# Retention operands of a hybrid encoder block: split before they are stored, or after they are loaded

## The chip, the core and the metric

The kernel runs on one core of one Trainium2 chip. Five engines work side by side, each with its own instruction queue in program order: TensorE (PE, with its weight loads shown as PEld), VectorE (DVE), ScalarE (ACT), GpSimd (POOL) and SyncE (SP), which here only issues DMAs. The metric is the device time of one launch in microseconds, as the median of several runs. One further execution was profiled, and the views of its trace are what the text reads.

## The reference

One encoder layer over 2048 rows of width 1024. After an RMS norm one matrix product gives ten groups of columns. Branch A is a banded attention over chunks of 64 rows. Branch B is a retention with 8 heads, keys of width 64 and values of width 128. Both are gated, projected, merged, projected again, added to the input and normed. What the change touches is branch B:

```python
qr = rotary(q_r.reshape(B, S, R_HEADS, R_KEY_DIM), positions)
kr = rotary(k_r.reshape(B, S, R_HEADS, R_KEY_DIM), positions)
o_r = retention_chunkwise(qr, kr, v_r.reshape(B, S, R_HEADS, R_VAL_DIM), gn_gain[l])
...
s = jnp.einsum('bnqhd,bnkhd->bnhqk', qc, kc) * intra_decay
o_intra = jnp.einsum('bnhqk,bnkhe->bnqhe', s, vc)
kv = jnp.einsum('bnkhd,hk,bnkhe->nbhde', kc, state_decay, vc).astype(jnp.float32)
...
return state * chunk_decay[None, :, None, None] + kv_n, state
...
mean = jnp.mean(o, axis=-1, keepdims=True)
var = jnp.mean(jnp.square(o - mean), axis=-1, keepdims=True)
o = (o - mean) * lax.rsqrt(var + GN_EPS)
```

Rotated queries and keys make scores, scores and a running state make the output, and each head's output is normed over its 128 values. The kernel centres the values over these 128 ahead of time, so that the output needs no mean.

## The kernel before

**Numbers in two halves.** Matrix products take operands in the type fp32r, which holds fewer bits than fp32. To keep the accuracy, an operand is split: the high half is a cast to fp32r on ScalarE, the low half is the fp32 number less the high half, on VectorE or GpSimd. A product of two split numbers is three matmuls, or two where the halves of one operand lie under each other in the partitions.

**Stages.** The rows are handled in two halves s = 0, 1 of 1024 rows, two blocks b of 512 rows in each. For every half the stages are: the projection of queries, keys and values (`p0`, `p1`: 14 chunks of 256 columns, by a Strassen scheme of seven products), attention, and retention. The projections of the gates (`g0`, `g1`) run along with attention and retention: their products are cut into steps of three matmuls of 512 columns, and `fill(n)` (L497) puts n such steps between the parts of attention or retention. A credit carries fractions over, so 1.9 means 19 steps in ten fills. At the end come the merge and the output projection.

**Deferred work.** `later(n, fn)` (L242) defers a piece of work by n steps; `step()` (L487) first emits what is due, then the next three matmuls. `put(lag, dst, src)` is a deferred store. `emit` takes the earliest piece out of the list, and `sure(cond)` (L1493) emits pieces in order until its condition holds. In these stages every engine keeps the order in which the pieces are emitted; all DMAs but the weight loads are issued on SP, in that order.

**Buffers.** The pool `E` holds tiles of 128 x 512 fp32, 23 of them in a projection and 22 in retention (`E_PROJ`, `E_RET`). An instruction that writes a new tile waits until its buffer's last use is over; for a load that wait stands in SP's queue. PSUM has four banks `ACC`, shared by the gate products and the kv update.

**Queries and values before they are stored.** A block of rotated queries is two tiles `xs` (first and second half of the rotary pairs). `parted` (L936) casts each to a high half, makes the low half, and stores both: four stores of 256 KB for a block and a group of four heads. Values: `ep_vr` (L985) transposes them, subtracts the mean (`centred`), casts the high half on ScalarE (`high`), makes the low half on GpSimd (`low`), and stores both: two stores of 256 KB for a head and a block.

**Retention** (`retention`, L1364) goes through `todo`: for each pair p of heads four steps st of 256 rows. An item is one head i of a step. `load_scored` loads keys `kr`, queries `qr` (each row twice, once under the other, since the keys' halves lie so) and, at a pair's first step, the masks `dm`. `load_valued` loads decayed keys `kd` and values `vr`. For each item, `scores` makes the matmuls into `sr`, then `sm` = `sr` times the mask on VectorE, `sh` its high half on ScalarE and `sl` its low half on GpSimd; they are used two items, or four fills, later by `output`. `update` makes the matmuls `kv`, and its `added` brings them into `state` [64 x 256]: at st = 0 ScalarE copies, else VectorE scales and adds, and then VectorE adds three more parts. Three steps later ScalarE casts the high half of the state into `sstk`, one step later VectorE makes the low half. In the first half's last step of a pair (st = 3) the state is stored to `sts` and `sks` for the second half, three steps later still. `evacuate` takes the output from PSUM, squares it and sums the squares on TensorE (`ssq`). The loop at L1568 sets the order:

```python
if st < 7:
    update(p, st)
if m + 1 < len(todo):
    load_valued(*todo[m + 1])
```

Both stand at a step's start (i = 0), ahead of the fill; the scored loads of the step after next stand at the end of its first item.

Of the kernel before, what the change touches and what calls it, by code (L numbers as in the profile page):

```python
# [21 lines left out]
P = 128  # L22
# [48 lines left out]
def hybrid_kernel(  # L71
# [881 lines left out]
    def queries(cc, b, xs, nm, late):  # L953
        parted(xs, nm, late + 9, dve, lambda i, h: r32(qrscr[cc][b][:, :, :, h, i]).rearrange("u i c t -> (i c) u t"))
# [30 lines left out]
    def ep_vr(cc, b, j, src, ps):  # L985
# [4 lines left out]
        def rest():  # L990
# [4 lines left out]
            vv = []  # L995
# [17 lines left out]
            later(4, high)  # L1013
            later(6, low)
# [349 lines left out]
    def retention(s, ps_ret):  # L1364
# [8 lines left out]
        def load_scored(p, st):  # L1373
# [5 lines left out]
            qs = []  # L1379
# [5 lines left out]
            for i in range(2):  # L1385
                q = E(f"qr_{nm}_{i}", F32R, (P, 2, T))
                for half in range(2):
                    dma(
                        r32(q[64 * half:64 * half + 64]),
                        r32(qrscr[cc][b][un, 2 * (p % 2) + i]).rearrange("c h n t -> (c h) n t"),  # L1390
                    )
                qs.append(q)
                if st == 4 * s:
                    load_mask(p, i)
            tiles[p, st] = ks, qs

        def load_valued(p, st):

            b, un = st // 2, st % 2
            nm = f"{p}_{st}"  # L1400
            kd = E(f"kd_{nm}", F32R, (P, 2, T))
            dma(r32(kd), r32(kdscr[p][b][:, un]))
            vs = []
            for i in range(2):
                v = E(f"vr_{nm}_{i}", F32R, (P, 2, 2 * DV))
                dma(
                    r32(v), r32(vrscr[2 * p + i][b][:, 2 * un:2 * un + 2]).rearrange("p t n d -> p t (n d)")
                )
                vs.append(v)
            values[p, st] = vs, kd.rearrange("p i (t c) -> p i t c", t=2)  # L1410

# [11 lines left out]

        def scores(p, st, i):

            nm = f"{p}_{st}_{i}"
            ks, qs = tiles[p, st]
            sp = ps_ret.tile([P, 512], F32, tag="sr", bufs=2, name=f"sr_{nm}")
            for kk in range(2):
                o = sp[:, kk * T:(kk + 1) * T]  # L1430
                kcol = ks[:, i, kk * P:(kk + 1) * P]
                pe.matmul(o, kcol, qs[i][:, 0, :], start=True, stop=False)
                pe.matmul(o, kcol, qs[i][:, 1, :], start=False, stop=True)
# [19 lines left out]
        def update(p, st):  # L1453

            vs, kd = values[p, st]
            kv = ACC(f"kv_{p}_{st}")
# [36 lines left out]
        def sure(here):  # L1493

            while not here():
                emit()

        def output(p, st, i, parts, ops):
            qs, vs = tiles[p, st][1], values[p, st][0]
            o = ops[:, i * T:(i + 1) * T]  # L1500
            sure(lambda: len(parts) == 2 and (st == 0 or (p, st) in sstks))
# [284 lines left out]
```

## Time and profile before

| what | us |
|---|---|
| median of 3 runs | 1989.13 (1988.7 to 1997.05) |
| the profiled execution: time | 1994.13 |
| the profiled execution: span of the trace | 1992.3 |
| mean granted TensorE clock | 0.994 |
| DMA issues `qr<-qrs`, x128 of 128 KB: median to landing | 4.4 |
| DMA issues `vr<-vrs`, x64 of 256 KB: median to landing | 5.3 |
| bytes moved by DMA | 447.45 MB, mean 225 GB/s |

A view's row names engine, operation, and what it writes and reads by the program's tile names; `x64` counts instructions. Nearly all rows carry line 140, that of the helper through which every engine call goes, so instructions are told apart by their tiles. Tiles that end in `_p` and `_g` belong to the q/k/v and gate projections. The retention stages lie at about 590 to 780 and 1365 to 1565 us from the start of the span, the two q/k/v projections at 0 to 366 and 780 to 1130.

### The profile page before, as it was taken

How to read it: one execution, taken by the hardware profiler on the slowest of the kernel's cores; microseconds unless marked ns; L12 is line 12 of the kernel's file. 1: busy time of each engine (PE TensorE's matmuls, PEld its weight loads, DVE VectorE, ACT ScalarE, POOL GpSimd, SP SyncE). 2: the span in 40 equal slices, each digit the busy share in tenths (PEclk: the TensorE clock that was granted, in tenths of full speed). 3: DMA queues.
4: the chain of work that ended last, by engine and by line, in shares of the span. 5: the costliest groups of instructions: out<-in, count | busy, mean ns of one | idle time of the engine just before them, and what ended most of it. 6: DMA issues, size and time to landing. Idle time of an engine off the chain costs nothing.

```text
span 1992.3 us, 30382 instructions
## 1 busy us (share of the span) xinstructions
PE 1927.1 (97%) x9712; PEld 1606.7 (81%) x9712; DVE 1362.2 (68%) x2613; ACT 900.4 (45%) x1827; POOL 853.0 (43%) x703
## 2 busy tenths in 40 slices
PE   6899999999999999999999999999999999999998
PEld 4677788888887877787788888888888887888886
DVE  7887878677765658889887677765557653544554
ACT  6454554566654545443333555654455311322221
POOL 2343544555546665555553444444665144021000
PEclk9999999999999999999999999999999999999999
DMA  4576795756549987687785646554998999976564
GB/s 148 156 265 186 226 307 196 213 153 183 161 132 268 289 243 250 214 289 230 231 277 173 190 150 176 157 144 141 275 285 283 334 377 360 341 242 216 193 193 138
DMA packets 341967, 447.45 MB, mean 225 GB/s; under 512 B 30808, under 2 KB 195312, under 8 KB 341808
## 3 DMA queue, kind: packets, MB, share of 16 engines
q1 hardware_dynamic: 284800, 389.92, 61.3%
q10 hardware_dynamic: 57008, 55.59, 9.2%
q8 instruction: 78, 1.28, 0.3%
q14 instruction: 81, 0.66, 0.1%
HBM read 294.50 MB, written 150.89 MB: 224 GB/s over the span
## 4 chain that ended last, share of the span: by engine, by line
PE 52%; DMA 6%; DVE 6%; issue 2%; POOL 1%; SPq 1%; ACT 0%; DVEq 0%; ACTq 0%; POOLq 0%
PE ps_g_z L140 4%; PE ps_g_x L140 4%; PE ps_p_z L140 3%; PE o L140 2%; PE po L140 2%; PE ps_p_x L140 2%; PE ps_g_v L140 2%; PE ps_g_w L140 2%; PE ps_g_y L140 2%; PE wide L140 2%; PE tp L140 1%; PE ps_p_y L140 1%; PE sr L140 1%; PE ps_p_w L140 1%; PE ps_p_v L140 1%
## 5 line engine op out<-in xcount | busy, mean ns | idle before, releaser
L140 POOL TENSOR_SCALAR pr<-pr,rsum 128x640 f32<-128x640 f32 (+4 forms) x128 | 96.0, 750 | 225.9 <-DVE ptl L140 105.7
L140 PE MATMUL ps_p_z<-r,wh_p 128*128 128x512 f32 x448 | 142.7, 400 | 7.0 <-DVE c_p L140 4.5
L140 PE MATMUL ps_g_z<-r,wh_g 128*128 128x512 f32 x448 | 143.9, 403 | 4.0 <-DVE c_g L140 4.0
L140 PE MATMUL ps_g_x<-r,wh_g 128*128 128x512 f32 x448 | 142.7, 400 | 1.9 <-ACT u_g L140 1.9
L140 PE MATMUL ps_p_x<-r,wh_p 128*128 128x512 f32 x448 | 142.3, 399 | 1.4 <-ACT u_p L140 1.4
L140 DVE CUSTOM_DVE_ANT_0 pr<-wide,bt 128x640 f32<-128x640 f32 (+4 forms) x128 | 94.3, 737 | 71.2 <-PE wide L140 65.4
L140 ACT ACTIVATE pr<-pr,mn 128x640 f32<-128x640 f32 (+4 forms) x128 | 98.0, 766 | 84.9 <-DVE mn L140 84.9
L140 POOL TENSOR_TENSOR t_p<-raw_p,t_p 128x512 f32<-128x512 f32 x50 | 74.5, 1491 | 130.1 <-DVE wl_p L140 114.9
L140 DVE TENSOR_TENSOR ptl<-tp,pth 128x384 fp32r<-128x384 f32 x168 | 96.0, 573 | 40.8 <-ACT pth L140 40.5
L140 ACT CAST pth<-tp 128x384 fp32r<-128x384 f32 x168 | 84.7, 516 | 70.0 <-PE tp L140 64.5
L140 DVE TENSOR_TENSOR wl_p<-t_p,wh_p 128x512 fp32r<-128x512 f32 x112 | 106.4, 951 | 2.0 <-ACT wh_p L140 2.0
L140 POOL TENSOR_TENSOR sl<-sm,sh 128x512 fp32r<-128x512 f32 x64 | 87.7, 1371 | 44.3 <-ACT sh L140 27.5
L1122 POOL TENSOR_TENSOR gr<-gr,ta 128x512 f32<-128x512 f32 x32 | 44.6, 1395 | 141.8 <-DVE gr L1121 133.3
L140 PEld LDWEIGHTS ps_p_z<-r,wh_p 128*128 128x128 f32 x448 | 82.5, 190 | 24.7 <-issue 7.2
L140 PEld LDWEIGHTS ps_p_x<-r,wh_p 128*128 128x128 f32 x448 | 83.8, 190 | 19.9 <-ACT u_p L140 2.2
L140 PE MATMUL wide<-ka,qa 128*128 128x512 f32 (+2 forms) x448 | 94.4, 326 | 2.3 <-DVE mn L140 2.3
L140 DVE TENSOR_TENSOR sm<-sr,dm 128x512 f32<-128x512 f32 x64 | 44.1, 690 | 71.9 <-PE sr L140 41.3
L140 PEld LDWEIGHTS tp<-ident,pr 128*128 128x128 f32 x560 | 71.3, 140 | 27.1 <-POOL pr L140 2.2
L140 POOL TENSOR_TENSOR wl_g<-t_g,wh_g 128x512 fp32r<-128x512 f32 x56 | 75.0, 1339 | 42.3 <-ACT wh_g L140 31.4
L140 PE MATMUL po<-pth,va 128*128 128x256 f32 x336 | 93.1, 298 | 0.0
L140 PE MATMUL tp<-ident,pr 128*128 128x128 f32 x560 | 89.0, 272 | 2.9 <-POOL pr L140 1.6
L140 ACT CAST wh_p<-t_p 128x512 fp32r<-128x512 f32 x112 | 69.1, 619 | 48.1 <-PE ps_p_z L140 19.5
(1184 smaller groups left out, 5879.2 us busy)
## 6 DMA issues: line engine op xcount, KB each, us to landing
raw_g<-in_w_in_dram ACTq DMA_DIRECT2D x56, 512.0 KB, 5.4
raw_p<-in_w_in_dram ACTq DMA_DIRECT2D x50, 512.0 KB, 6.4
qa<-qas SPq DMA_DIRECT2D x128, 128.0 KB, 3.1
qr<-qrs SPq DMA_DIRECT2D x128, 128.0 KB, 4.4
vr<-vrs SPq DMA_DIRECT2D x64, 256.0 KB, 5.3
ka<-kas SPq DMA_DIRECT2D x40, 256.0 KB, 3.7
va<-vas SPq DMA_DIRECT2D x40, 256.0 KB, 3.4
kds<-kdt_k SPq DMA_DIRECT2D x32, 256.0 KB, 4.4
```

Source lines behind the costliest of these rows:

```text
L140: return tc.keep_in_program_order(op(*a, **k))
L1122: pool.tensor_tensor(g, g, ta, ALU.add)
```

## The change

Queries and values are stored whole, as fp32, and split in retention after they are loaded. A query tile now holds both heads of a pair, each row twice as before, and is split into a high tile (ScalarE) and a low one in place (VectorE); values come as one tile for both heads, and their high halves (ScalarE) and low halves (VectorE) go into two tiles. The splits are deferred by 7 or 8 steps from the load, and by more at retention's start; `sure` now also guards scores, update and output until the splits are emitted. Values of the step after next are loaded at the end of a step, scored loads at a step's start. The update's matmuls come behind the fill. `state` is set to zero by GpSimd at a pair's start in place of ScalarE's copy, and VectorE makes both halves of the state at once behind the sums. The diff, cut to its core:

```diff
-    qrscr = [[D(f"qrs_{c}_{b}", [2, 4, 32, 2, 2, T], F32R) for b in range(NB)] for c in range(2)]
+    qrscr = [[D(f"qrs_{c}_{b}", [2, 2, 32, 2, 2, T]) for b in range(NB)] for c in range(2)]
-    vrscr = [[D(f"vrs_{h}_{b}", [P, 4, 2, DV], F32R) for b in range(NB)] for h in range(HEADS)]
+    vrscr = [[D(f"vrs_{h}_{b}", [P, 4, DV]) for b in range(NB)] for h in range(HEADS)]
...
     def queries(cc, b, xs, nm, late):
-        parted(xs, nm, late + 9, dve, lambda i, h: r32(qrscr[cc][b][:, :, :, h, i]).rearrange("u i c t -> (i c) u t"))
+        def store(n, i):
+            src = xs[n][32 * i:32 * i + 32].rearrange("c (u t) -> c u t", u=2)
+            dma(qrscr[cc][b][:, i // 2, :, n, i % 2].rearrange("u c t -> c u t"), src)
+        for n in range(2):
+            for i in range(4):
+                later(late + 8 + PUT + n, lambda n=n, i=i: store(n, i))
...
-            def high():
-                vv.extend(two(f"vr_{nm}", (P, 4, DV)))
-                act.copy(vv[0], vc)
-            def low():
-                pool.tensor_tensor(vv[1], vc, r32(vv[0]), ALU.subtract)
-                for n in range(2):
-                    put(PUT, r32(vrscr[h][b][:, :, n, :]), r32(vv[n]))
+                put(PUT, vrscr[h][b], vc)
...
-        def load_scored(p, st):
+        def load_scored(p, st, more=0):
...
+            ql = E(f"qr_{nm}", F32R, (P, 2, T))
+            for half in range(2):
+                dma(
+                    r32(ql[64 * half:64 * half + 64]),
+                    qrscr[cc][b][un, p % 2].rearrange("c h i t -> (c h) i t"),
+                )
...
+            def high():
+                qs.append(E(f"qh_{nm}", F32R, (P, 2, T)))
+                act.copy(qs[0], r32(ql))
+                later(2, low)
+            def low():
+                dve.tensor_tensor(ql, r32(ql), r32(qs[0]), ALU.subtract)
+                qs.append(ql)
+            later(8 + more, high)
-        def load_valued(p, st):
+        def load_valued(p, st, more=0):
...
+            raw = E(f"vr_{nm}", shape=(P, 2, 2, DV))
+            for i in range(2):
+                dma(raw[:, i], vrscr[2 * p + i][b][:, 2 * un:2 * un + 2])
...
+            def high():
+                ws = [E(f"v_{nm}_{i}", F32R, (P, 2, 2 * DV)) for i in range(2)]
+                for i in range(2):
+                    act.copy(ws[i][:, :, 0:DV], raw[:, i])
+                later(2, lambda: low(ws))
+            def low(ws):
+                for i in range(2):
+                    dve.tensor_tensor(ws[i][:, :, DV:2 * DV], raw[:, i], r32(ws[i][:, :, 0:DV]), ALU.subtract)
+                vs.extend(ws)
+            later(7 + more, high)
...
             def added():
                 for i in range(2):
-                    if st == 0:
-                        act.copy(state[:, i, :], kvv[0:64, i, 0:DV])
-                        continue
...
-                later(3, lambda: high(sstk))
-            def high(sstk):
-                act.copy(sstk[0:64], state)
-                later(1, lambda: low(sstk))
-            def low(sstk):
+                dve.tensor_copy(sstk[0:64], state)
                 dve.tensor_tensor(sstk[64:128], state, r32(sstk[0:64]), ALU.subtract)
                 if st == 3:
                     put(3, stscr[p], state.rearrange("p i c -> p (i c)"))
...
-        load_scored(*todo[0])
-        load_valued(*todo[0])
-        load_scored(*todo[1])
+        load_scored(*todo[0], 3)
+        load_valued(*todo[0], 5)
+        load_scored(*todo[1], 5)
         load_state(*todo[0])
+        load_valued(*todo[1], 9)
+        load_scored(*todo[2], 9)
...
-                if st < 7:
-                    update(p, st)
                 if m + 1 < len(todo):
-                    load_valued(*todo[m + 1])
                     load_state(*todo[m + 1])
+                if m and m + 2 < len(todo):
+                    load_scored(*todo[m + 2])
             fill(RET_FILL)
+            if i == 0 and st < 7:
+                if st == 0:
+                    pool.memset(state, 0.0)
+                update(p, st)
...
-            if i == 0 and m + 2 < len(todo):
-                load_scored(*todo[m + 2])
+            if i == 1 and m + 2 < len(todo):
+                load_valued(*todo[m + 2])
             fill(RET_FILL)
```

More of the change, by code (lines that the diff above doesn't have):

```diff
@@ L1422, in load_mask, with sure @@
             dma(dms[p][i], dmask[2 * p + i])
+        def sure(here):
+            while not here():
+                emit()
         def scores(p, st, i):
@@ L1431, in scores @@
                 kcol = ks[:, i, kk * P:(kk + 1) * P]
-                pe.matmul(o, kcol, qs[i][:, 0, :], start=True, stop=False)
-                pe.matmul(o, kcol, qs[i][:, 1, :], start=False, stop=True)
+                pe.matmul(o, kcol, qs[0][:, i, :], start=True, stop=False)
+                pe.matmul(o, kcol, qs[1][:, i, :], start=False, stop=True)
             got = []
@@ L1500, in output @@
             o = ops[:, i * T:(i + 1) * T]
-            sure(lambda: len(parts) == 2 and (st == 0 or (p, st) in sstks))
+            sure(lambda: len(parts) == 2 and len(vs) == 2 and (st == 0 or (p, st) in sstks))
             sh, sl = parts
@@ L1504, in output @@
                 sstk = sstks[p, st]
-                pe.matmul(o, sstk[:, i, :], qs[i][:, 0, :], start=True, stop=False)
-                pe.matmul(o, sstk[:, i, :], qs[i][:, 1, :], start=False, stop=False)
+                pe.matmul(o, sstk[:, i, :], qs[0][:, i, :], start=True, stop=False)
+                pe.matmul(o, sstk[:, i, :], qs[1][:, i, :], start=False, stop=False)
             for kk in range(2):
```

27 lines of the change are left out of this document (5 added, 22 removed).

## The prediction

> **What bounds the kernel now.** First the head of the page: which engine is full. Then the busy time of each engine in long stretches that follow the stages (columns: stretch, length, busy time and instructions of PE, PEld, DVE, ACT and POOL, granted clock, DMA share, GB/s).
>
> ```profile
> span 1992.3 us, 30382 instructions
> PE 1927.1 (97%) x9712; PEld 1606.7 (81%) x9712; DVE 1362.2 (68%) x2613; ACT 900.4 (45%) x1827; POOL 853.0 (43%) x703
> ```
>
> ```profile
> 20.00:366.00 346.00, 329.56 (x1523) 266.03 (x1522) 274.68 (x405) 178.01 (x375) 149.25 (x102) 0.99 0.66 209
> 590.00:780.00 190.00, 180.07 (x1009) 154.12 (x1007) 114.77 (x194) 93.84 (x181) 112.95 (x84) 0.99 0.84 254
> 780.00:1130.00 350.00, 340.52 (x1569) 278.15 (x1570) 293.96 (x405) 145.60 (x277) 181.36 (x127) 1.00 0.75 239
> 1365.00:1565.00 200.00, 197.91 (x1114) 170.37 (x1113) 122.48 (x207) 101.20 (x188) 112.67 (x84) 1.00 0.86 267
> ```
>
> TensorE bounds it: it is idle for 65 us of 1992. The change leaves every matmul and touches four stages: the two q/k/v projections (20 to 366 and 780 to 1130), where work goes, and the two retentions (590 to 780 and 1365 to 1565), where work comes. There PE is idle for 16.4, 9.5, 9.9 and 2.1 us. So 38 us, part of it start-up, is all that could be won; the question is how much of it this change ends, and how much it makes. Next, what PE waited for: three rows of the whole run, five of the first retention, one of the second (us, times, longest).
>
> ```profile
> PE ps_p_z L140 <- DVE c_p L140: 4.5, 4, 1.6
> PE trva L140 <- DVE c_p L140: 2.4, 3, 1.1
> PE ps_p_w L140 <- DVE wl_p L140: 2.1, 3, 1.0
> ```
>
> ```profile
> PE ps_g_z L140 <- DVE c_g L140: 2.1, 1, 2.1
> PE ps_g_x L140 <- ACT u_g L140: 1.9, 2, 1.2
> PE o L140 <- POOL sl L140: 1.7, 3, 1.0
> PE kv L140 <- DMA vr<-vrs: 1.3, 2, 0.8
> PE ssq L140 <- POOL o2l L140: 1.1, 1, 1.1
> ```
>
> ```profile
> PE kv L140 <- DMA vr<-vrs: 0.4, 1, 0.4
> ```
>
> The longest is 2.1 us at 723; the timeline (start, length, idle before and its releaser) tells why.
>
> ```profile
> 710.69 3.16 SPq L140 DMA_DIRECT2D qr<-qrs  x4
> ...
> 716.44 0.47 SPq L140 DMA_DIRECT2D sts<-state  x1
> ...
> 720.59 0.42 ACT L140 COPY state<-kv 64x128 f32<-64x128 f32 x2 [3.82 <-DMA sts<-state]
> 721.04 1.33 DVE L140 TENSOR_TENSOR state<-kv,state 64x256 f32<-64x256 f32 x3 [5.29 <-ACT state L140]
> ...
> 723.15 0.74 PE L140 MATMUL ps_g_z<-r,wh_g 128*128 128x512 f32 x2 [2.06 <-DVE c_g L140]
> ```
>
> A new head pair starts. ScalarE's copy into `state` must wait until the store of the last pair's state has read it; VectorE waits for ScalarE, the gate sum c_g stands behind VectorE's state parts, and PE waits for c_g. The other rows I need give retention's rate: two kv updates four steps apart, an output beside them, and two stretches.
>
> ```profile
> 661.49 0.48 PE kv L140 x4
> ...
> 663.34 0.96 PE o L140 x8
> ...
> 696.82 0.48 PE kv L140 x4
> ```
>
> ```profile
> 660.00:700.00 40.00, 40.00 (x244) 35.37 (x244) 23.29 (x46) 22.84 (x46) 27.11 (x22) 1.00 0.93 283
> 720.00:740.00 20.00, 17.94 (x100) 15.53 (x99) 13.17 (x25) 11.67 (x23) 9.52 (x7) 0.91 0.75 225
> ```
>
> A step (one pair, 256 rows) takes (696.82 - 661.49)/4 = 8.83 us; sixteen take 141 us. Where PE never idles (660 to 700), VectorE is busy for 58%, or 5.14 us of a step, and DMA for 93%.
>
> **The change part by part.** *Store wait at a new pair.* The store was due 1+3+1+3 = 8 steps behind the update, the next pair's first sum 8.6 behind it (four fills of 1.9, and one): no room. (These are steps of the projection, 7.6 to a retention step.) Now VectorE does both halves at once, so the store is due after 4 and the memset that must wait for it after 7.6: 3.6 steps of 8.83/7.6 us = 4.2 us later, and the store above took 720.59 - 716.44 = 4.1 us. I count the wait as gone: 2.06 us, and with it the lower clock behind it, 0.09 of 20 us (0.91 in that slice) = 1.8 us. Gain 3.9 us, bounds 0 and 3.9. If the SP queue is late, GpSimd waits in ScalarE's place (a rival).
>
> The Trainium skill ("TensorE: Matmul & The Clock Gate", What's actually happening) has the clock fall after an idle window of about 3.4 us. Here the slice behind an idle time of 2.06 us has 0.91. By the page alone this part would be worth 2.1 us and not 3.9; the measurement decides.
>
> *Loads issued earlier.* Scores' loads move ahead of a fill, and so ahead of that fill's gate and output stores on SP; these stores free buffers only. Four query loads took SP 3.16 us above, two remain, 1.6 us less a step, which pays for it. Values are asked for at the end of the step two before their use. The kv waits, 1.3 + 0.4 = 1.7 us, go; their splits are due 9 steps after the load, 2.4 before use, so these hide. Gain 1.7, bounds 0 and 1.7.
>
> ```profile
> L140 DVE TENSOR_TENSOR l_q<-u_p,h_q 128x512 fp32r<-128x512 f32 x8 | 5.4, 679 | 0.0
> L140 POOL TENSOR_TENSOR l_vr<-u_p,h_vr 128x512 fp32r<-128x512 f32 x16 | 21.1, 1320 | 0.0
> L140 ACT CAST h_vr<-u_p 128x512 fp32r<-128x512 f32 x16 | 9.9, 620 | 12.9 <-DVE u_p L140 12.9
> ```
>
> *Projections relieved.* Out go 16 splits of queries and 32 of values: on VectorE 16 x 0.68 = 11 us, on GpSimd 32 x 1.32 = 42 us, on ScalarE 48 x 0.62 = 30 us, half of each per projection. VectorE holds PE up there for 4.5 + 2.4 + 2.1 = 9.0 us. It loses 11 of 569 us, and GpSimd, which makes it wait, 42 of 331. I take a quarter of the 9.0: gain 2.3, bounds 0 and 9.0. Query stores go from 4 to 8 per block of 512 rows and column group, value stores from 2 to 1 per head: with two groups and eight heads SP has 24 a block before and after.
>
> *DMA.* 64 of the 128 query loads of 128 KB go, the 64 value loads halve, the stores halve: 8.4 + 8.4 + 4.2 + 8.4 = 29 MB of 447. In the rows above PE waits for DMA at kv alone. So this is worth nothing beyond the two parts above, unless the full queue causes more than its rows say.
>
> *Splits that come into retention.* For VectorE per step: one query low half (128x512), two value low halves (128x256), one state copy (64x256); at a pair's first step also two scaled adds in place of copies. None of these is in retention's trace; the nearest rows, 600 to 757:
>
> ```profile
> L140 DVE TENSOR_TENSOR wl_g<-raw_g,wh_g 128x512 fp32r<-128x512 f32 x14 | 12.8, 912 | 0.0
> L140 DVE TENSOR_TENSOR state<-kv,state 64x256 f32<-64x256 f32 x48 | 20.3, 423 | 11.6 <-ACT state L140 10.1
> L140 DVE TENSOR_TENSOR sstk<-state,sstk 64x256 fp32r<-64x256 f32 x16 | 10.4, 650 | 1.6 <-ACT sstk L140 1.2
> L140 DVE SCALAR_TENSOR_TENSOR state<-state,kv 64x128 f32<-64x128 f32 x24 | 5.7, 274 | 8.5 <-PE kv L140 8.5
> ```
>
> The query half: 0.68 (l_q) to 0.91; I take 0.91, the same shape in the same stage. A value half has 256 columns and two SBUF operands like sstk: 0.42 to 0.65, I take 0.65, twice. The copy: 0.2 (half of 0.42) to 0.65, I take 0.42. The adds: 2 x 0.27 in one step of four, 0.14. Together 0.91 + 1.30 + 0.42 + 0.14 = 2.8 us (1.9 to 3.5 if every SBUF operation meets GpSimd as the worst of these did): VectorE goes from 58% to 7.9/8.83 = 90%. ScalarE gets three casts for one, at most 3 x 0.62 = 1.9 us a step: from 57% (22.84 of 40) to at most 78%; not the bound.
>
> The Trainium skill ("SBUF — State Buffer", Who interferes with whom) says why 0.65 and not 0.42: a VectorE operation with two SBUF operands and a GpSimd operation that reads SBUF lock each other out, one with a PSUM operand does not. The rows agree (650 against 423 ns). It speaks against this change: all four new operations would be of the blocking sort, and by it GpSimd would be held up too, a cost that my sum leaves out.
>
> What does 90% cost? PE against VectorE in the second projection:
>
> ```profile
> 780.00:830.00 50.00, 46.58 (x192) 36.75 (x193) 48.97 (x55) 28.03 (x51) 32.83 (x20) 0.97 0.72 237
> 830.00:1030.00 200.00, 195.74 (x902) 160.04 (x901) 173.83 (x228) 74.86 (x142) 109.03 (x73) 1.00 0.82 266
> ```
>
> ```profile
> 1525.00:1545.00 20.00, 19.71 (x115) 16.78 (x113) 18.84 (x29) 12.69 (x26) 10.18 (x6) 1.00 0.85 279
> ```
>
> At 87% PE idles 4.26 of 200 us, 2.1%; at 98%, 3.42 of 50, 6.8%. Thirty-two steps are about 295 us: 2.1% is 6.2 us. Of the waits that stay (1.9 + 1.7 + 1.1) some are the same ones, so loss 4.0, bounds 0 and 20. The second retention's end is at 94% already: loss 1.0, bounds 0 and 3.
>
> *The query split is tight in the first retention.* Scores come 5 fills x 1.9 = 9.5 steps after the load, the low half is due after 10. In about half of the 16 steps it is issued directly ahead of the scores. If a gate sum (0.69) stands before it on VectorE, PE comes 0.69 + 0.91 - 0.96 (the output) = 0.64 us early. Products end every fourth step: between 2 and 4 such meetings, loss 1.5, bounds 0 and 8 x 0.64 = 5.1. With 2.2 a fill in the second retention there is room.
>
> Sum: -3.9 - 1.7 - 2.3 + 4.0 + 1.0 + 1.5 = **-1.4 us** on the profiled 1994.13 (span 1992.3 and 1.8 around it), which lies 5.0 above the median of the runs, 1989.13. From the median: **1987.7**.
>
> **The rivals.** *A: the queue costs more than its rows say.* SP's loads and stores are in order, DMA stands at 93%; with fewer of them ScalarE and GpSimd get theirs earlier too, and the other waits of the first retention (1.9 + 1.7 + 1.1 = 4.7) go as well, while VectorE's 42% of free time takes the splits. For it: nearly all retention's waits sit in the first, with three new pairs. Against: none of the 4.7 names a DMA. 7.9 + 4.7 = 12.6 less: 1976.5.
>
> *B, slower: VectorE fills up.* Place: retention's steps, where state sums, gate sums and masks queue behind the splits. It decides from 98% on: 0.98 x 8.83 - 5.14 = 3.5 us added a step, the upper end above. Price 6.8% of 295 = 20.1, less the 7.9: 2001.3. Against: the masks' results are used four fills later.
>
> *C: the wait moves to GpSimd.* If the state store is issued 4 us late (SP blocked by a load without a free buffer), the memset waits, and the score low halves behind it on GpSimd, and PE for these. The gain of 3.9 is lost, and two more pairs stall alike: -1.4 + 3 x 3.9 = +10.3: 1999.4.
>
> *D: the loads are issued sooner but do not start sooner*, because they wait for a free buffer of the 22: kv's 1.7 stays: 1989.4.
>
> **How the numbers follow.** Forecast 0.44, A 0.24, B 0.18, C 0.06, D 0.08. About 0.5% (10 us) is what a measurement of this kernel can tell from no change. Faster than that: A, 0.24. Within: forecast and D, 0.52. Slower: B and C, 0.24. The range goes to the middle of A and of B and a little beyond: 1974 to 2002.
>
> **What would show it.** VectorE's share in 660 to 700 near 90% (under 80% speaks for A, 97% for B); no PE wait for vr at kv; no long wait of VectorE for `state` at a new pair, and a memset on GpSimd that waits for the store would be C; 418 MB moved, DMA share in retention near 0.75; fewer PE waits for c_p in the projections; short PE waits of the scores (sr) for VectorE in the first retention alone. Wrong would be the forecast if PE's idle time in the two retentions together left the stretch from 4 to 18 us.

## The result, and the profile after

| | before | after |
|---|---|---|
| median of 5 runs, us | 1989.13 | 2008.01 |
| lowest to highest, us | 1988.03 to 1997.05 | 2006.79 to 2008.88 |
| the profiled execution: time, us | 1994.13 | 2008.28 |
| its span, us | 1992.3 | 2006.4 |

The ratio is 1.0087, with a 95% interval of 1.0067 to 1.0106: slower by 0.9%. The forecast was 1987.7, its range 1974 to 2002, so the time lies outside the range, on the side of rival B. The head of the page of the changed kernel, and the same long stretches as before:

```profile
span 2006.4 us, 30244 instructions
PE 1935.0 (96%) x9712; PEld 1611.6 (80%) x9712; DVE 1437.5 (72%) x2729; ACT 897.0 (45%) x1839; POOL 817.2 (41%) x675
```

```profile
20.00:366.00 346.00, 331.52 (x1530) 267.63 (x1530) 270.73 (x398) 164.75 (x351) 126.33 (x86) 0.99 0.60 192
590.00:780.00 190.00, 176.53 (x975) 150.04 (x974) 161.25 (x255) 100.80 (x200) 116.08 (x87) 0.98 0.65 202
780.00:1130.00 350.00, 340.34 (x1560) 277.69 (x1559) 284.82 (x394) 130.83 (x249) 159.62 (x112) 1.00 0.68 220
1365.00:1565.00 200.00, 192.84 (x1082) 166.48 (x1081) 153.73 (x259) 112.06 (x219) 117.28 (x85) 0.97 0.67 205
660.00:700.00 40.00, 37.96 (x222) 32.57 (x221) 35.62 (x61) 21.33 (x42) 24.62 (x19) 1.00 0.66 203
```

In the projections (rows 1 and 3) VectorE, ScalarE and GpSimd have less work than before. In the retentions (rows 2 and 4) VectorE went from 115 and 122 us to 161 and 154, and the granted clock fell to 0.98 and 0.97. Fixed stretches of time don't hold the same work in two kernels, though. So the stages are cut at events: from the first scores (`sr`) of a retention to its last. These two stretches, first in the kernel before and then in the changed one:

```profile
599.20:746.90 147.70, 139.74 (x820) 121.06 (x819) 86.31 (x155) 74.82 (x147) 94.65 (x72) 0.99 0.89 266
1389.20:1540.40 151.20, 150.26 (x881) 131.00 (x880) 94.91 (x157) 79.85 (x149) 96.14 (x71) 1.00 0.93 283
```

```profile
597.80:754.60 156.80, 144.00 (x819) 123.18 (x818) 137.26 (x224) 83.07 (x167) 99.19 (x76) 0.98 0.64 197
1395.80:1556.30 160.50, 154.30 (x880) 134.20 (x879) 133.97 (x219) 94.78 (x187) 102.58 (x72) 0.97 0.71 219
```

The retentions got longer by 9.1 and 9.3 us. The rest of the span got shorter by 4.3 (1.4 before the first retention, 1.1 up to the second attention, 1.8 behind the second retention), and 9.1 + 9.3 - 4.3 is the 14.1 us between the two spans. So all the loss sits in the retentions. It has two halves: PE's idle time rose by 4.8 (156.80 - 144.00 against 147.70 - 139.74) and 5.3 us, and PE's *busy* time by 4.3 and 4.0 with the same matmuls (a few of them fall on the other side of a cut). What PE waited for, the first retention (590 to 780) and then the second (1365 to 1565 and a little beyond):

```profile
PE sr L140 <- DVE qr L140: 7.8, 8, 2.1
PE kv L140 <- DVE v L140: 2.4, 3, 0.9
PE o L140 <- ACT o L140: 1.5, 2, 1.3
```

```profile
PE sr L140 <- DVE qr L140: 3.7, 2, 3.3
PE ps_g_x L140 <- ACT u_g L140: 2.5, 1, 2.5
```

The waits of before (c_g at the new pair, DMA at kv) are gone, and new ones stand there: scores for the low half of the queries, kv for the low half of the values. Most of the second half is slower matmuls. They are seen in the timeline of PE behind one of these waits, and not behind the next:

```profile
645.87 0.39 PE L140 MATMUL sr<-qr,kr 128*128 128x256 f32 x1 [1.74 <-DVE qr L140]
...
646.33 1.03 PE L140 MATMUL ps_g_z<-r,wh_g 128*128 128x512 f32 x2
647.15 0.63 PE L140 MATMUL ps_g_z<-r,wl_g 128*128 128x512 f32 x1
```

```profile
658.41 0.39 PE L140 MATMUL sr<-qr,kr 128*128 128x256 f32 x1 [1.60 <-DVE qr L140]
...
658.87 0.62 PE L140 MATMUL ps_g_z<-r,wh_g 128*128 128x512 f32 x2
659.32 0.39 PE L140 MATMUL ps_g_z<-r,wl_g 128*128 128x512 f32 x1
```

Two matmuls take 0.62 us at the full clock and 1.03 at the lower one, which held until 649.7. Four slices of 20 us of the two retentions have a lower clock, 0.91, 0.91, 0.91 and 0.83: 1.8 + 1.8 + 1.8 + 3.4 = 8.8 us, against 1.8 in one slice of before. So about 7.0 of the 8.3 us are the clock's.

What VectorE has to do more is told by its groups in the first retention. One group that both kernels have (before, then after), and the groups that are new or longer:

```profile
L140 DVE TENSOR_TENSOR sm<-sr,dm 128x512 f32<-128x512 f32 x31 | 21.4, 690 | 37.8 <-PE sr L140 17.6 <-DMA ors<-oz 9.6 <-PE kv L140 6.1
```

```profile
L140 DVE TENSOR_TENSOR v<-vr,v 128x256 fp32r<-128x256 f32 x30 | 21.7, 764 | 1.2 <-ACT v L140 1.2
L140 DVE TENSOR_TENSOR sm<-sr,dm 128x512 f32<-128x512 f32 x31 | 21.3, 688 | 3.2 <-PE sr L140 2.4
L140 DVE TENSOR_TENSOR qr<-qr,qh 128x512 fp32r<-128x512 f32 x16 | 18.5, 1158 | 3.9 <-ACT qh L140 3.9
L140 DVE TENSOR_TENSOR sstk<-state,sstk 64x256 fp32r<-64x256 f32 x15 | 14.1, 941 | 0.5
L140 DVE CAST sstk<-state 64x256 fp32r<-64x256 f32 x15 | 9.2, 616 | 0.5
```

Look at the idle time in the `sm` rows, the masks. Before, VectorE stood idle for 37.8 us ahead of them, mostly waiting for PE: a mask was made as soon as its scores were there. After, 3.2 us: the masks stand in a queue. ScalarE, which makes the score halves, waits longer for them (first retention, before and after):

```profile
ACT sh L140 <- DVE sm L140: 21.8, 11, 6.0
```

```profile
ACT sh L140 <- DVE sm L140: 42.3, 13, 5.5
```

This alone did not hold PE: of its 12.8 us of idle time 10.2 name the low halves of queries and values (7.8 + 2.4), and 0.7 GpSimd's score halves `sl`. What stands ahead of a late low half is seen at the second of the two scores above (VectorE, with the GpSimd operation that runs beside it); the last line is a query split of another step:

```profile
655.29 0.69 DVE L140 TENSOR_TENSOR u_g<-ps_g_w,u_g 128x512 f32<-128x512 f32 x1 [1.07 <-PE ps_g_w L140]
655.90 0.77 DVE L140 TENSOR_TENSOR wl_g<-t_g,wh_g 128x512 fp32r<-128x512 f32 x1
656.08 1.73 POOL L140 TENSOR_TENSOR sl<-sm,sh 128x512 fp32r<-128x512 f32 x1
656.60 1.76 DVE L140 TENSOR_TENSOR qr<-qr,qh 128x512 fp32r<-128x512 f32 x1
...
696.06 0.68 DVE L140 TENSOR_TENSOR qr<-qr,qh 128x512 fp32r<-128x512 f32 x1
```

Two things delay it that the busy share of VectorE hides. First, order: VectorE had just stood idle for 1.07 us, because the gate sum at the head of its queue waited for PE's own products; ScalarE's high half had been ready since 654.2. In the first retention four of the six score waits of over 0.4 us have such an idle time of 0.9 to 1.4 us shortly ahead of them.

Second, GpSimd: the subtraction took 1.76 us and not 0.68. Of the 16 query splits of the first retention, the 7 that started while GpSimd was not in the middle of an operation took 0.68 or 0.69 us, the 9 that started while it was took 1.18 to 1.78. The waits of 1.74, 1.60, 2.11 and 1.02 us all stand behind one of 1.75 to 1.78. If all of the four SBUF groups above (`v`, `qr` and the two of `sstk`) had taken their shortest times (0.41, 0.68, 0.42 and 0.28 us), VectorE would have been busy for an estimated 30 us less of its 137.

The queue itself, at the second retention's end, where the wait is longest (the changed kernel's timeline, VectorE with PE and one ScalarE row between):

```profile
1541.89 0.63 ACT L140 CAST qh<-qr 128x512 fp32r<-128x512 f32 x1
...
1545.22 0.28 PE L140 MATMUL sr<-qh,kr 128*128 128x256 f32 x1
1545.80 1.16 DVE L140 TENSOR_TENSOR r<-r,r 128x512 fp32r<-128x512 f32 x1
1546.88 0.68 DVE L140 TENSOR_TENSOR wl_ba_(0, 0)_17646<-raw_ba,wh_ba_(0, 0)_17645 128x512 fp32r<-128x512 f32 x1
1547.48 0.68 DVE L140 TENSOR_TENSOR r<-r,r 128x512 fp32r<-128x512 f32 x1
1548.08 0.68 DVE L140 TENSOR_TENSOR qr<-qr,qh 128x512 fp32r<-128x512 f32 x1
1548.82 0.58 PE L140 MATMUL sr<-qr,kr 128*128 128x256 f32 x1 [3.31 <-DVE qr L140]
```

ScalarE had made the queries' high half by 1542.52 (1541.89 + 0.63). The low half starts 5.6 us later, behind the merge's splits (`r`, `wl_ba`), and PE stands at the scores. At the second retention's start it is ScalarE's order that stops PE:

```profile
1392.20 6.19 SPq L140 DMA_DIRECT2D qr<-qrs  x2
...
1401.71 0.62 ACT L140 CAST qh<-qr 128x512 fp32r<-128x512 f32 x1 [5.31 <-DMA qr<-qrs]
1402.23 0.58 ACT L140 COPY u_g<-ps_g_x 128x512 f32<-128x512 f32 x1
...
1402.87 0.74 PE L140 MATMUL ps_g_x<-r,wh_g 128*128 128x512 f32 x2 [2.47 <-ACT u_g L140]
```

The cast waits for its load, the copy of a gate product out of PSUM stands behind the cast, and PE waits for that bank. Between these two ends the second retention runs almost without loss. Its three parts in the changed kernel:

```profile
1396.00:1416.00 20.00, 17.53 (x87) 14.69 (x87) 14.86 (x21) 8.97 (x19) 11.71 (x9) 0.91 0.66 194
1416.00:1536.00 120.00, 119.59 (x710) 104.95 (x709) 101.59 (x167) 74.72 (x147) 84.26 (x60) 1.00 0.75 233
1536.00:1556.00 20.00, 16.69 (x84) 14.13 (x83) 17.51 (x31) 10.76 (x22) 6.37 (x5) 0.83 0.52 159
```

With VectorE at 101.59/120 = 85% PE idles 0.4 us in 120.

### The profile page after: what moved, and what is told of

The parts are those of the page before. It is cut to its first block, busy times and chain, and to the rows that moved or that the text cites. A ratio compares the mean times of both kernels' runs of the same rounds, so it can differ in the third digit from the quotient of the medians.

```text
span 2006.4 us, 30244 instructions
## 1 busy us (share of the span) xinstructions
PE 1935.0 (96%) x9712; PEld 1611.6 (80%) x9712; DVE 1437.5 (72%) x2729; ACT 897.0 (45%) x1839; POOL 817.2 (41%) x675
## 2 busy tenths in 40 slices
DMA packets 304079, 418.07 MB, mean 208 GB/s; under 512 B 29785, under 2 KB 165617, under 8 KB 303921
## 4 chain that ended last, share of the span: by engine, by line
PE 72%; DVE 12%; DMA 9%; issue 3%; ACT 1%; SPq 1%; POOL 0%; DVEq 0%; ACTq 0%; POOLq 0%
PE ps_g_z L140 6%; PE ps_g_x L140 6%; PE ps_p_z L140 5%; PE ps_p_x L140 5%; PE po L140 4%; PE wide L140 3%; PE ps_g_v L140 3%; PE ps_g_w L140 3%; PE ps_g_y L140 3%; PE tp L140 2%; PE ps_p_y L140 2%; PE ps_p_v L140 2%; PE ps_p_w L140 2%; PE o L140 2%; DVE wl_p L140 2%
## 5 line engine op out<-in xcount | busy, mean ns | idle before, releaser
L140 PEld LDWEIGHTS wide<-ka,qa 128*128 128x128 f32 x448 | 75.3, 188 | 19.0 <-DVE mn L140 7.4
```

The lines of the kernel that those rows point to most:

```text
L140: return tc.keep_in_program_order(op(*a, **k))
```

## The experiments

Each ratio is to the kernel before, in runs on the same chip, with its 95% interval; the stretches are those of the two retentions as above (147.7 and 151.2 before, 156.8 and 160.5 after) in one profiled execution each. The span of one kernel differs by some 5 us between executions, so the stretches show places, and the ratios decide.

**Splits four steps sooner** (x1_earlier). The first pair of lines is that of the queries, the second that of the values. If the new waits are only a matter of position, this ends them.

```diff
-            later(8 + more, high)
+            later(4 + more, high)
-            later(7 + more, high)
+            later(3 + more, high)
```

> Only the deferral of the splits changes: queries 4 steps behind the load in place of 8, values 3 in place of 7. The same work on every engine. Position theory (the low halves are issued so close ahead of the matmuls that use them that VectorE's backlog falls on PE): the waits of sr for qr (7.8 us in the first retention, 3.7 in the second) and of kv for v (2.4) go, and with them the halved clock behind them (about 8 us of slower matmuls): 1990 to 1996 us. Load theory (VectorE is too full, and the backlog only shows up at another wait): 2003 to 2009, VectorE's share in retention unchanged near 86%, other waits of PE for VectorE or for the score halves in their place.

1.0119 [1.0100, 1.0138], 162.0 and 161.9 us: slower still, and above both ranges. The waits of scores for `qr` and of kv for `v` are gone, but PE now waits for ScalarE: `o` 6.8 and `u_g` 6.1 us in the first retention, 4.8 and 7.8 in the second. The casts come ahead of their loads: ScalarE waits for `qr` 13.6 and 21.4 us, where it was 5.3 and 7.1 in the changed kernel.

**The low halves on GpSimd**, of the values (x2_vpool) and of the queries (x3_qpool): in the one line of each subtraction `dve` becomes `pool`.

> The low halves of the values go from VectorE to GpSimd (1.5 us of VectorE's 8.6 a step; two operations of 128x256 more on GpSimd). Load theory: VectorE falls to about 72% of the retention, PE's waits for qr shrink with the backlog by half or more: 1995 to 2001. Position theory: the waits of kv for v go, but the query half still stands directly ahead of the scores: 2001 to 2006. If GpSimd becomes the bound (65% and about 1.4 us a step more), o waits for sl: 2008 or above.

> The low half of the queries goes from VectorE to GpSimd (1.16 us of VectorE a step, some 1.3 us more on GpSimd). Load theory: VectorE falls to about 74%, the waits of sr turn into shorter ones for GpSimd: 1997 to 2003. Position theory: the half is still issued directly ahead of its use, now behind GpSimd's score halves: the waits of sr stay at 10 us or grow, 2004 to 2012.

x2: 1.0080 [1.0065, 1.0095], 157.9 and 162.3 us. VectorE's share in the first retention falls to 124.42/157.90 = 79%, and the scores still wait 9.0 and 4.1 us for `qr`, whose subtraction, with more GpSimd work beside it, now takes 1418 ns on average in place of 1158. The time was forecast for a GpSimd that has become the bound, but only 1.9 us of PE's idle time in the first retention name its `sl`. x3: 1.0064 [1.0048, 1.0081], 157.3 and 158.9; PE waits for GpSimd's `qr` (4.2) and `sl` (3.8) and for `v` (3.7). GpSimd has no room for the work either: with the queries its busy time in the first retention is 118.98 of 157.30 us.

**More and fewer buffers** (x5_e24, x6_e20): `E_RET = 24` (with `CS = 5` and `PARTS = 7`, which give up the room) and `E_RET = 20`.

> The changed kernel with 24 buffers in retention in place of 22; the space comes from one output tile (6 to 5) and one weight-part tile (8 to 7) of the dense products. Buffer theory (the loads, issued half a step sooner, stand in SP's queue until one of the 22 buffers is free, and so the casts on ScalarE and the low halves come late): the waits of SP for sl, ssq, o and sm (42 us in the first retention) fall by half, PE's waits for qr and u_g too: 1996 to 2002. Load theory (VectorE is full, whenever the loads land): retention as long as in the changed kernel within 2 us each, 2006 to 2012, with a little lost in the projections for the tiles taken away.

> The changed kernel with 20 buffers in retention. Buffer theory: every load starts later still, ScalarE's casts wait for them with the gate work behind: 2020 to 2035. Load theory: 2006 to 2011.

The retentions take 157.0 and 160.7 us with 24 buffers, 157.0 and 163.6 with 20, 156.8 and 160.5 with 22. So they don't hang on the buffers. The whole is 1.0206 [1.0172, 1.0240] with 24, nearly all of it behind the second retention (475.3 us against 450.1), presumably for the tiles that the dense products gave up, and 1.0070 [1.0047, 1.0092] with 20.

**One part at a time.** x4_state is the kernel before with the change's `update` alone: the memset, VectorE's two halves of the state, the matmuls behind the fill. x7_q_as_before and x8_v_as_before are the changed kernel with the queries, or the values, split before they are stored, as in the kernel before. Of x7, the part in retention:

```diff
-            ql = E(f"qr_{nm}", F32R, (P, 2, T))
...
-            later(8 + more, high)
+            for i in range(2):
+                q = E(f"qr_{nm}_{i}", F32R, (P, 2, T))
...
+                qs.append(q)
```

> The kernel before with the state part of the change alone: update's matmuls behind the fill, memset by GpSimd in place of ScalarE's copy, both halves of the state at once on VectorE. Queries and values are split before they are stored, as before. By the prediction's sum 3.9 us less than before (the wait for the state store and the lower clock behind it go): 1984 to 1987. By the rival that the wait moves to GpSimd: no gain or up to 8 us more, 1989 to 1997.

> The changed kernel with the queries split before they are stored, as before, and loaded in halves; values whole, state part and loading order stay changed. Load and position theories: the waits of sr for qr (7.8 + 3.7 us) and the clock lost behind them go, VectorE falls from 86 to about 74%: 1990 to 1996. Buffer theory: the queries take as many buffers as in the changed kernel, and the loads are longer, so the loads stay late: 1998 to 2006.

> The changed kernel with the values split before they are stored, as before; queries whole, state part and loading order stay changed. Load theory: VectorE falls by 1.5 us of 8.6 a step to about 71%, the waits of sr for qr fall with its backlog to under half: 1993 to 1999. Position theory: the query half stays directly ahead of the scores: 2000 to 2006. Buffer theory: a step takes one buffer less and holds it shorter, SP waits less: 1996 to 2003.

x4: 1.0003 [0.9989, 1.0017], neither gain nor loss. In its profiled execution the first retention takes 143.8 us, 3.9 less than before and just the gain that was forecast; the second takes 7.7 more. That execution, at 2000.0 us, was the slowest of x4's ten, 5.2 above their median, so it leaves open whether the state part costs anything there. x7: 0.9999 [0.9979, 1.0018], 147.2 and 154.3: with the queries split before the store the whole loss is gone, within the interval, though the values are still split in retention. x8: 1.0027 [1.0012, 1.0041], 150.0 and 160.2: a third of the loss is left. The two sorts of splits add up to more than each alone (0.0087 against 0.0027 with queries alone and 0 with values alone). That fits a queue that fills up better than a price per split.

**Where the query split stands.** x9_q6: at 6 steps in place of 8, and later for the one load at the start (`load_scored(*todo[1], 9)`). x10_q_ahead: keys and queries loaded three steps ahead in place of two, split 12 steps after.

> The changed kernel with the queries' split 6 steps behind their load in place of 8 (4 was the first experiment), and 4 steps later than in the changed kernel for the second load of a retention. Squeeze theory (PE waits where the split is issued right ahead of the scores; ScalarE is held up where the cast stands ahead of the load's landing): the sr waits for qr fall below 4 us in all, ScalarE's waits for qr stay below 8 us: 1996 to 2003. Load theory (VectorE is full): 2005 to 2010.

> The changed kernel with keys and queries loaded a whole step sooner (three steps ahead in place of two) and split 12 steps behind the load, so about 3 steps of the projection ahead of the scores; the same work. Squeeze theory: neither PE nor ScalarE waits for a query in the steady steps: 1991 to 1999. Load theory: 2005 to 2010. If the 22 buffers bind after all (two more tiles live): later loads, 2005 or above.

x9: 1.0064 [1.0041, 1.0087], 155.1 and 159.3 us. The scores' waits fall from 7.8 + 3.7 to 0.4 + 1.5, and others come: `o` for `sh` 5.3 and 5.2, kv for `v` 3.3. x10: 1.0113 [1.0090, 1.0136], 162.2 and 167.6; the scores wait 0.4, kv 7.6 and `ssq` 5.2 in the first retention, and the cast of `qh`, which needs a buffer of its own, waits for one (10.8 us for GpSimd's `o2l`). So the wait at the scores is where the queue shows, not why it is there: taken away, the time comes back elsewhere.

**The same work, used by nobody** (x11_unused_split): x7, whose queries come already split, with a cast and a subtraction of 128x512 a step whose result is read by nothing.

```diff
+            def high():
+                idle = E(f"qi_{nm}", F32R, (P, 2, T))
+                act.copy(idle, r32(qs[0]))
+                later(2, lambda: low(idle))
+            def low(idle):
+                dve.tensor_tensor(idle, r32(qs[0]), r32(idle), ALU.subtract)
+            later(8 + more, high)
```

> The seventh experiment (queries stored and loaded in halves, which costs nothing against before) with the splits of the changed kernel added as unused work: the same cast on ScalarE and subtraction on VectorE of 128x512, at the same places behind the same load, into a tile that nothing reads. Load theory: the same VectorE and ScalarE work as in the changed kernel, so most of its loss, 2004 to 2012. Position theory: PE never waits for these two, so the sr waits of 11.5 us and their lower clock are not there; what stays is ScalarE held up by a late load at the second retention's start: 1994 to 2001.

1.0056 [1.0038, 1.0075], 155.8 and 153.5 us. PE never waits for the unused halves; it waits for kv's `v` (5.2) and for ScalarE's `o` and `sh` (2.8 + 2.5) in the first retention. About two thirds of the loss is made by the work alone, and in the profiled execution nearly all of that lies in the first retention (155.8 of the changed kernel's 156.8). Of the second's 9.3 us only 2.3 are left: there most of the loss seems to need the waits for the queries themselves.

**Which of the two** (x12_unused_cast: the cast alone; x13_unused_sub: the subtraction alone, of the two query tiles).

> The kernel with queries split before they are stored, and of the unused split only its cast (one ScalarE cast of 128 x 512 a step, into a tile that nothing reads). With cast and subtraction unused the ratio was 1.0056, with neither 0.9999. If it is VectorE's load that costs, this one stays within 1.0 +- 0.002 (the retentions at 147 and 154 us); if it is ScalarE's order (a cast that waits for its load, with gate copies and score halves behind it), it keeps most of the loss: 1.004 or more.

> The same with only an unused VectorE subtraction of 128 x 512 a step (of the two query tiles, into a tile that nothing reads). If VectorE's load costs: 1.004 or more, first retention 153 us or more. If ScalarE's order costs: within 1.0 +- 0.002. If each costs half: both near 1.0028.

The two retentions of x12 and then of x13 (length; PE, PEld, DVE, ACT, POOL; clock, DMA share, GB/s):

```profile
598.70:746.20 147.50, 141.32 (x820) 123.10 (x819) 123.38 (x208) 82.80 (x167) 96.84 (x76) 0.98 0.80 240
1389.10:1542.40 153.30, 150.12 (x881) 131.15 (x880) 122.61 (x196) 92.83 (x183) 97.83 (x71) 1.00 0.84 253
```

```profile
601.00:757.20 156.20, 143.80 (x820) 123.14 (x819) 137.51 (x224) 75.64 (x152) 100.40 (x76) 0.98 0.76 227
1399.20:1560.70 161.50, 152.98 (x881) 132.51 (x880) 138.77 (x217) 84.64 (x169) 99.41 (x71) 0.99 0.80 243
```

x12: 1.0027 [1.0014, 1.0040]. x13: 1.0097 [1.0070, 1.0125]. Neither settles the question. By the ratios the cast is worth 0.0028 (x12 against x7) and the subtraction beside it 0.0029 (x11 against x12): half each, the third of the possibilities written down. By the profiled executions the cast costs nothing (the retentions of x12 are as long as those of x7), and the subtraction 8.3 us in the first retention (155.8 in x11 against 147.5), where it takes VectorE from 84 to 88% of the stage. x13 does less work than x11 and loses more, as much as the whole change, with ScalarE at 75.6 us as in the kernel before. But its subtraction also waits for the queries' load itself (8.8 us in the first retention), with all of VectorE's queue behind it; in the changed kernel the cast on ScalarE does that. So x13 shows what a late load does at the head of VectorE's queue, and not the price of a subtraction. That VectorE's work alone makes the loss is likely for the first retention, and not shown.

**More matmuls beside each step** (x14_after_fill is the changed kernel, x15_before_fill the kernel before): `RET_FILLS = (2.0, 2.5)` in place of `(1.9, 2.2)`. A bigger part of the gates' products then runs in retention, above all in the second, and VectorE has more time for each step.

> The changed kernel with 2.0 and 2.5 projection steps a fill in place of 1.9 and 2.2: more matmuls between retention's parts, so that the load per time falls, by 13% of the matmuls of the gate in the second retention, and 5% in the first. If the loss is the load of the steps, the second retention loses less against the kernel before with the same fills than the 9.3 us it lost: 5 or less. If it is something that each step costs whatever its length, it stays at 9.

> The control: the kernel before with the same fills (2.0, 2.5). Its retentions are longer by their extra matmuls, what lies behind them shorter; no more than 0.3% either way is expected of the whole.

The control x15, then x14:

```profile
599.10:741.20 142.10, 141.32 (x840) 123.93 (x839) 88.30 (x157) 75.22 (x149) 96.08 (x74) 1.00 0.91 280
1381.60:1546.20 164.60, 162.94 (x938) 141.91 (x936) 98.27 (x167) 85.18 (x159) 96.02 (x72) 1.00 0.90 274
```

```profile
597.50:747.50 150.00, 145.07 (x840) 124.98 (x839) 135.91 (x225) 84.88 (x172) 100.10 (x76) 1.00 0.69 208
1388.70:1553.80 165.10, 162.89 (x937) 141.90 (x936) 140.70 (x226) 96.89 (x194) 100.15 (x72) 1.00 0.75 234
```

x15: 0.9985 [0.9975, 0.9995]; x14: 1.0009 [0.9996, 1.0021]. The change now costs 1994.91 - 1989.28 = 5.6 us of the medians, 0.3%, in place of 0.9%. In the second retention, which got 14% more gate steps a fill, 165.1 against 164.6 us: the loss of 9.3 is down to 0.5, with VectorE at 85% of the stage (140.70/165.10) where it was at 83%. In the first, with 5% more, 150.0 against 142.1: 7.9 are left, and VectorE is at 91% there (135.91/150.00). What went in the second are its two ends: the wait at the start is 1.6 us, with the clock at 1.00 behind it, and there is none for `qr` at the end. The middle had lost only 0.4 us with 2.2 steps already. So the same splits can be nearly free; whether the longer steps or the shifted ends made them so, these two runs do not separate. Nor is all of a rise in PE's busy time the clock: in x14's first retention it is 3.8 us above the control's, at a granted clock of 1.00.

**Both remedies together** (x16_q_before_fill: x7 with these fills).

> The changed kernel with queries split before they are stored and with 2.0 and 2.5 projection steps a fill. The parts gave 0.9999 (queries) and 0.9985 (the fills on the kernel before). If the remaining parts of the change are worth nothing, 0.9985; if its small gains (the state store's wait, the earlier loads) show where VectorE has room, 0.996 or less.

1.0036 [1.0024, 1.0048], 149.7 and 166.8 us: a miss. The forecast was 0.9985 or less, and VectorE has room (83% and 80%). It is also slower than x14 (1.0009 [0.9996, 1.0021]), which splits the queries after the load: with these fills, taking the query split out of retention gained nothing. PE waits for GpSimd's `sl`, 3.3 us in six times in the first retention (0.8 in the control); why the score halves come late there is open. The best of all versions is x15, the kernel before with more fill, by 0.15%.

## Why the prediction was wrong

**The load was right as a share, and too low as a time.** VectorE's share in 660 to 700 was forecast at 90%, and is 35.62/40 = 89%; 418 MB were forecast, 418.07 were moved. The new and longer operations cost, over the first retention, 18.5 + 21.7 + 9.2 + (14.1 - 10.0 for the low halves of the state) + 1.9 (the scaled adds) = 55.4 us, 3.5 a step where 2.8 was taken: the query half is 1.16 and not 0.91, a value half 0.76 and not 0.65, the copy 0.62 and not 0.42. VectorE's busy time as a whole rose by 51.0 us there, 3.2 a step, and by 39.1 in the second retention, 2.4 a step. That the share fits is in part luck: more work stands in a longer step (137.26/16 = 8.6 of 156.80/16 = 9.8 us, where 7.9 of 8.83 was forecast).

The prediction cited the Trainium skill ("SBUF — State Buffer", Who interferes with whom) for operations with two SBUF operands and a GpSimd operation that shut each other out. The trace agrees: the query split takes 0.68 us, or 1.18 to 1.78 when it starts behind a running GpSimd operation; the low half of the state went from 665 to 941 ns in the first retention; and the sums of the state, which have an operand in PSUM, stayed at 423 ns. The prediction took one mean, 0.91 us, for a time that is either short or long.

**The step that failed is the price of that load** ("What does 90% cost?": +4.0 us, bounds 0 and 20, with the second retention's end at +1.0, bounds 0 and 3). It was read from the second projection, where PE idles 2.1% with VectorE at 87%. The retentions lost 9.1 + 9.3 = 18.4 us of 298.9, or 6.2%: three times as much. All terms that lie in them were forecast at -3.9 - 1.7 + 4.0 + 1.0 + 1.5 = +0.9. The prediction's own sign of being wrong came true: PE's idle time in its two stretches is 13.47 + 7.16 = 20.6 us, outside 4 to 18. Two things were missed. First, idle time is only part of it. Of the 18.4 us, 10.1 are idle time and about 7.0 the lower clock behind the stalls. The prediction counted the clock once, behind the stall that it removed, and never behind those that it added, though its row with VectorE at 98% has a clock of 0.97. Second, a share says how much VectorE has to do, not in which order, nor how long an operation stands behind GpSimd. At 85% the middle of the second retention loses 0.4 us in 120; its two ends lose nearly all of the 9.3, and of these only the later one (3.31 us idle, 3.4 of clock) hangs on VectorE. The earlier one (2.47 and 1.8) is ScalarE's order, behind a late load. No run takes the meetings with GpSimd away and leaves the rest, so how much of the loss they make is open.

**Rival B, "VectorE fills up", came nearest.** Its price, 20.1 us, is close to the 18.4, in part by luck: it was read at 98%, and VectorE was at 88 and 83% of the two stages. Its time, 2001.3, was still 6.7 short of the 2008.0, as it kept 7.9 of gains. The point from which it decides was wrong (98%, or 3.5 us added a step), and the place only half right. It had state sums, gate sums and masks queue behind the splits; PE's waits name the splits, behind gate sums and weight parts. Against it stood that "the masks' results are used four fills later", and that held in the main: ScalarE's waits for masks doubled (21.8 to 42.3 us), but in x4 they are 60.5 us in a first retention that lost nothing.

**The query split** was priced at 1.5 us (0 to 5.1), for the first retention alone, and "with 2.2 a fill in the second retention there is room". Scores waited 7.8 us in the first, above the upper bound: a meeting was taken at 0.64 us, with a subtraction of 0.91, and the four long ones are 1.0 to 2.1, with subtractions of 1.75 to 1.78. They waited 3.3 in one wait in the second, where it was VectorE's queue and not the due time that was late. Yet this term was no separate cost: with the scores' waits gone (x9, x10) the kernel was not faster.

**The gains.** The wait at the new pair went as forecast, and no memset waited long (rival C was not seen). But x4, which has this part alone, measures 1.0003. The forecast 3.9 us would be 0.998, and its interval ends at 0.9989, or 2.2 us: the wait was gone in its first retention, and the whole gained less than that. The kv waits for DMA went too, and came back as waits for VectorE's `v` (2.4 against 1.7): the sentence "so these hide" was wrong for the values. The projections' relief of 2.3 us agrees with what the two got shorter by, 1.4 + 1.1, in one execution each. ScalarE was called "not the bound" at 78%; on average, at 53 and 59%, it isn't, but in order it can be: a cast issued ahead of its load's arrival held PE for 2.47 us.

**Rival A** (the queue costs more than its rows say) did not decide: DMA's share went from 0.89 to 0.64 in the first retention, and the stage got longer. Its other waits did shrink there, from 4.7 to 1.4 us (`u_g` 0.7, `sl` 0.7, none for `o2l`), but PE was held elsewhere, and no run takes the transfers away without adding splits. So what A is worth by itself is not shown. **D** fell: the kv waits for DMA are gone, and 20, 22 or 24 buffers (x5, x6) give retentions of nearly the same length.

What stays open is x16, which is 0.5% slower than its control with VectorE at 80 to 83%, and how the loss divides among VectorE's work, its meetings with GpSimd and ScalarE's casts. A threshold in VectorE's share does not explain the runs: x2 loses 0.8% with VectorE at 79% of the first retention, and the first retention of x12 is as short as before with 84%. The longer subtractions of x2 are a likely reason there, and were not tried alone.

## What to carry to other kernels

Price work that is moved into a stage by who stands behind it in its engine's queue, not by that engine's share: add it to the time that each piece has before TensorE needs it, at its longest duration and not its mean (here 1.78 us and not 1.16), and allow for the lower clock behind a stall. Expect little of a transfer that is saved where no wait names it. A split after the load puts the wait for the load into a compute engine's queue. The price depends on what runs beside the splits: in the second retention they cost 9.3 us at 2.2 projection steps a fill and 0.5 at 2.5.

## What the hardware showed that was not expected

A stall of 1.74 us was followed by half the clock for the next 3.4 us (646.33 to 649.7), and so were those of 2.11, 2.47 and 3.31 us, while one of 1.60 us was not. The length does not decide this. In x5_e24 the same wait has the same length and leaves the clock alone:

```profile
647.66 0.39 PE L140 MATMUL sr<-qr,kr 128*128 128x256 f32 x1 [1.74 <-DVE qr L140]
...
648.13 0.63 PE L140 MATMUL ps_g_z<-r,wh_g 128*128 128x512 f32 x2
```

Stalls of 2.42 us (x11), 2.66 (x12) and 2.74 (x13) left it at 1.00 too, and one of 1.64 in x12, with 0.32 more just behind it, did not. The Trainium skill ("TensorE: Matmul & The Clock Gate", What's actually happening) names an idle window of about 3.4 us; here half of that was enough in some executions and not in others. Where it was, the stall cost about 1.7 us more, half of those 3.4.
